# A mixture-of-experts block on one core: the light part of each unit first, halves in another order, and the last norm by token tile

## The chip, the cores and the metric

The kernel runs on one core of a Trainium2 chip. The metric is the device time of one execution in microseconds (us); the figure given for a kernel is the median of its runs.

## What is computed

One decoder block on 512 tokens of width 1024, in float32. A mixer (state-space branch and short convolution) comes first and is not touched here. Then each token goes to 8 of 64 experts and to one shared expert, and the sum is normalised:

```python
def moe_ffn(h, ...):
    scores = jax.nn.sigmoid((hf @ router_w).astype(jnp.float32))
    ...
    _, e_idx = lax.top_k(jnp.where(expert_mask, biased, -jnp.inf), TOP_K)
    ...
    def expert_block(args):
        xb, e = args
        return (jax.nn.silu(xb @ w_gate[e]) * (xb @ w_up[e])) @ w_down[e]
    ...
    return (routed + shared).reshape(b, s, d)

x = (layer_norm(ALPHA * x + g2 * ffn) * ln2_g[l] + ln2_b[l]).astype(dtype)
```

An expert has gate and up weights of 1024 x 256 each and down weights of 256 x 1024: 3 MB in all, and every expert is read once.

## The kernel before

**Blocks.** Experts are ranked by how many tokens they got, and each rank has a fixed capacity (CAPS). A block is 128 token slots. A *full* block belongs to one expert. Its products are made in three passes of a fast format (matmul3, lines 153 to 155): the weights are split into a high part, which ACT copies (L158), and a low part, which DVE subtracts (L160); the parts go into a ring of three sets (wset, wring). A *tile* block is shared by two or four experts, 64 or 32 slots each, and multiplies the unsplit weights in float32, one column tile of TensorE per expert (tiled, L950).

**Units.** A unit is a group of blocks handled together. Its kind is written as letters: y is an expert of 192 slots (a full block, and a tile block it shares with an expert of 64), z the same with 160 slots and one of 32, x one of 320 slots (two full blocks and a tile block), f a full block, a a tile block for one expert of 96 slots and one of 32, p a tile block for two of 64, q a tile block for four of 32. ORDER lists the units; each letter is a *part* of its unit (a list in subs).

**Inside a unit** (ffn). The gate and up product of a block is cut into two halves along the width of the model, because weights arrive in pieces of 1 MB: a piece is half of an expert's gate and up weights, or all of its down weights. halves_of gives the order of parts, blocks and halves:

```python
return [(s_, 0) for s_ in subs] + [(s_[::-1], 1) for s_ in subs[::-1]]
```

So unit ya does: first half of y's full block, of y's tile block, of a; then second half of a, of y's tile block, of y's full block. Four tile halves in a row stand between two full halves. After a block's second half, act_in (L927, L928) applies the SiLU on ACT and the product on DVE. Then come the transposes of the result, the combination matmuls of the unit before (csteps, L1188 and L1189, added to the residual by DVE at L1194), the transposes of the next unit's tokens, and the down products in the order of the blocks, each followed by done (L1161, L1165, and a split).

**Order of loads.** The loop over units plans the pieces in the order of the halves, with the down pieces of a unit last; SyncE's queue issues them in that order (L869, L872). A piece goes into one of seven pair slots in turn, and every eighth into another pool (expert_piece), so a piece takes over the slot of the piece eight before it, and its load waits until that one was used for the last time. Tokens are gathered by POOL (L1132), three buffers ahead.

**Order on the engines.** From unit 1 on, TensorE follows the order of the program (manual_schedule); the other engines' orders are made by the framework's scheduler.

**The end.** After the last unit, combine(True) adds the last parts: per token tile and half, two matmuls (L1188, L1189) and one DVE addition from PSUM that also sums the row (L1191). Then finish runs the last norm by the list FORD: square (q: the mean at L1483 on DVE, the squared sum at L1484 on ACT), root (r: L1488 on ACT, L1489 on DVE; for token tile 0 also L1491 on DVE and L1492 on ACT), scale (s: L1497 and L1498 on DVE, for token tile 0 L1501 and L1502 on POOL) and the store (L1503). A loop for tokens beyond the capacities follows; it runs zero times on these inputs.

Of the kernel before, what the change touches and what calls it, by code (L numbers as in the profile page):

```python
# [8 lines left out]
F32 = mybir.dt.float32  # L9
# [3 lines left out]
AF = mybir.ActivationFunctionType  # L13
OP = mybir.AluOpType
# [4 lines left out]
T, D, P = 512, 1024, 128  # L19
# [18 lines left out]
NXG = 3  # L38


ORDER = "x ya qy za ap ya qff za ya ap faa za ap faa p"
AHEAD = 10
NDEF = 2
FORD = "q0 r0 s0 q1 r1 s1 q2 r2 s2 q3 r3 s3"
NADA = 3
ENG3 = ("PP", "VV", "VV", "VV")
NWK = 5
# [16 lines left out]
def block_kernel(ctx: ExitStack, tc: tile.TileContext, a, out, dbg=None):  # L64
# [43 lines left out]
    def page(shape, dt=F32, pool=None):  # L108
        n = 1
        for q in shape:  # L110
            n *= q
        assert n == 1024
        if pool or not pw:
            return (pool or pa).tile([P, *shape], dt, name="pg", tag="pg")
        if not halves:
            t = pair([2, 1024], dt)
            halves.extend((t[:, 1], t[:, 0]))
        return halves.pop()
# [13 lines left out]
    def bc_rows(ap, n, parts=P):  # L132
        return bass.AP(tensor=ap.tensor, offset=ap.offset, ap=[[0, parts], [1, n]])
# [818 lines left out]

    def halves_of(subs):

        return [(s_, 0) for s_ in subs] + [(s_[::-1], 1) for s_ in subs[::-1]]

    def ffn(blocks, subs, xs, w, done, gp=False):

# [48 lines left out]
    ra = []  # L1007
# [170 lines left out]
    def csteps(last=False):  # L1178

        ps_ = list(parts)  # L1180
        parts.clear()
        for t in range(NT):
            for n in range(2):
                ns_ = slice(n * 512, (n + 1) * 512)
                o = bank("y", 2)
                for i, (oht, yh, yl) in enumerate(ps_):
                    oh_ = oht[:, t * P:(t + 1) * P]
                    PE.matmul(o, oh_, yh[:, ns_], start=(i == 0), stop=False)  # L1188
                    PE.matmul(o, oh_, yl[:, ns_], start=False, stop=(i == len(ps_) - 1))  # L1189
                if last:  # L1190
                    V.scalar_tensor_tensor(ra[t][:, ns_], ra[t][:, ns_], 1.0, o, op0=OP.mult, op1=OP.add,  # L1191
                                           accum_out=rsum[:, t, n:n + 1])
                else:
                    V.tensor_tensor(ra[t][:, ns_], ra[t][:, ns_], o, op=OP.add)  # L1194
                yield

    def combine(last=False):
        for _ in csteps(last):
            pass

    out_proj(0)
# [206 lines left out]
    def unit(n):  # L1410
# [16 lines left out]
        tail[0] = n + 1 == len(units)  # L1427
        drain(run)

    over_ = iter(())  # L1430
    need_x(1)
    for n in range(MAN):
# [3 lines left out]
    with tc.manual_schedule(engines={mybir.EngineType.PE}):  # L1436
        for n in range(MAN, len(units)):
            unit(n)
        combine(True)
    ostart, oend, obase, nov = far  # L1440


# [26 lines left out]
        V.tensor_copy(po, pof)  # L1469
        return po, pv, ei  # L1470

    ln2g, ln2b = page([D]), page([D])
    SY.dma_start(ln2g, bc_rows(a["ln2_g"], D))
    SY.dma_start(ln2b, bc_rows(a["ln2_b"], D))

    def finish():

        os_, st = {}, {}

        def square(t):  # L1480
            os_[t] = page([D])
            st[t] = const.tile([P, 4], F32, name="fst", bufs=4)
            V.tensor_scalar(st[t][:, 0:1], rsum[:, t, 0:1], rsum[:, t, 1:2], -1.0 / D, op0=OP.add, op1=OP.mult)  # L1483
            S.activation(os_[t], ra[t], AF.Square, bias=st[t][:, 0:1], scale=1.0, accum_out=st[t][:, 1:2])  # L1484

        def root(t):
            nmu, ss, rs, nb = (st[t][:, i:i + 1] for i in range(4))
            S.activation(rs, ss, AF.Sqrt, bias=epsc, scale=1.0 / D)  # L1488
            V.reciprocal(rs, rs)  # L1489
            if ENG3[t] != "VV":  # L1490
                V.tensor_tensor(nb, nmu, rs, op=OP.mult)  # L1491
                S.activation(os_[t], ra[t], AF.Identity, bias=nb, scale=rs)  # L1492

        def scale(t):
            o, nmu, rs = os_[t], st[t][:, 0:1], st[t][:, 2:3]
            if ENG3[t] == "VV":
                V.scalar_tensor_tensor(o, ra[t], nmu, ln2g, op0=OP.add, op1=OP.mult)  # L1497
                V.scalar_tensor_tensor(o, o, rs, ln2b, op0=OP.mult, op1=OP.add)  # L1498
            else:
                e1, e2 = ({"V": V, "P": GP}[e] for e in ENG3[t])  # L1500
                e1.tensor_tensor(o, o, ln2g, op=OP.mult)  # L1501
                e2.tensor_tensor(o, o, ln2b, op=OP.add)  # L1502
            SY.dma_start(out[0, t * P:(t + 1) * P, :], o)  # L1503

        for c in FORD.split():
            {"q": square, "r": root, "s": scale}[c[0]](int(c[1]))

    finish()
    nv = nc.values_load(nov[0:1, 0:1], min_val=0, max_val=E + 32)
    with tc.For_i(0, nv, 1):  # L1510
        po, pv, ei = overflow(ocur)
        er = nc.values_load(ei[0:1, 0:1], engines=[mybir.EngineType.SP], min_val=0, max_val=E - 1)
        blk = slots((pv[:, :, None], P, [po]))
        drain(expert([[0]], [[0]], [blk], [xsplit(blk[0])], lambda e, q: expert_piece(bass.ds(er, 1), q)))
        combine(True)
        finish()
        V.tensor_scalar(ocur, ocur, 1.0, None, op0=OP.add)

# [23 lines left out]
```

## Time and profile before

| what | us |
|---|---|
| median of 3 runs | 1582.76 |
| lowest, highest | 1582.29, 1587.55 |
| the profiled execution's own time | 1580.36 |
| its span, first to last instruction | 1578.6 |
| TensorE busy in the span | 1486.1 (94%) |
| VectorE busy | 975.3 (62%) |
| ScalarE busy | 644.8 (41%) |
| GpSimd busy | 227.3 (14%) |

The engines are named PE (TensorE's matmuls), PEld (its weight loads), DVE (VectorE), ACT (ScalarE), POOL (GpSimd) and SP (SyncE); a q behind a name is the engine's sequencer. Times in the trace are us from the start of the span. Matmuls are pipelined, so PE can count as busy while it is partly waiting; the start of one group to the start of the next is the safer measure. PEclk is the granted clock of TensorE as a share of its full 2.4 GHz.

### The profile page before, as it was taken

Reading aid. Unit: us, or ns where it says so; the run is one execution under the profiler, and the core shown is the slowest. Engines: PE = TensorE matmul, PEld = TensorE weight load, DVE = VectorE, ACT = ScalarE, POOL = GpSimd, SP = SyncE. Lnnn points to the kernel's source line nnn. Section 1 sums busy time; section 2 is a strip of 40 time slices with the busy share of each in tenths; the row PEclk is TensorE's granted clock in tenths of the full one; section 3 lists DMA queues with packets and bytes.
Section 4 is the critical chain, followed back from the end, with each engine's and each line's share of the span. In section 5 each row is a group of like instructions: output and inputs, shape, how many; then the busy total and the mean of one; then the engine's idle time right before and its main releaser. Section 6 shows DMA issues by size and latency. Waiting matters only on the chain.

```text
span 1578.6 us, 22869 instructions
## 1 busy us (share of the span) xinstructions
PE 1486.1 (94%) x8253; PEld 1010.2 (64%) x8253; DVE 975.3 (62%) x1810; ACT 644.8 (41%) x925; POOL 227.3 (14%) x232
## 2 busy tenths in 40 slices
PE   6999989999999999999988999999988999999994
PEld 3688777787787886788766455555555554454552
DVE  4457786678767666635696666454566544563456
ACT  3456665575643445523353333232343322231222
POOL 0011110111010445700023300000000000000001
PEclk9999999999999999999999999999999999999997
DMA  9763423632531557634622967998989788997871
GB/s 278 183 158 91 104 67 84 151 77 80 151 88 37 170 178 231 202 101 148 228 84 92 370 224 260 375 383 296 345 299 349 293 332 336 353 365 282 319 286 55
DMA packets 194504, 335.67 MB, mean 213 GB/s; under 512 B 13428, under 2 KB 136660, under 8 KB 186196
## 3 DMA queue, kind: packets, MB, share of 16 engines
q1 hardware_dynamic: 183300, 303.73, 55.6%
q0 software_dynamic: 11088, 30.45, 7.4%
q8 instruction: 66, 1.08, 0.3%
q14 instruction: 50, 0.41, 0.1%
HBM read 334.58 MB, written 4.28 MB: 215 GB/s over the span
## 4 chain that ended last, share of the span: by engine, by line
PE 73%; DMA 11%; DVE 8%; ACT 3%; issue 2%; POOL 1%; SPq 1%; DVEq 0%; ACTq 0%; POOLq 0%
PE ps_pj L153 12%; PE ps_pj L154 12%; PE ps_pj L155 12%; PE ps_pj L950 8%; DMA pr<-in_w_up_dram 8%; PE ps_y L950 5%; PE ps_y L1188 5%; PE ps_y L1189 5%; PE ps_tr L150 4%; DMA pg<-in_w_ada_dram 2%; DVE wl L160 2%; PE ps_y L153 1%; PE ps_y L155 1%; PE ps_y L154 1%; PE ps_y L483 1%
## 5 line engine op out<-in xcount | busy, mean ns | idle before, releaser
L153 PE MATMUL ps_pj<-hm,wh 128*128 128x512 f32 x680 | 276.5, 408 | 1.0 <-ACT wh L158 0.9
L155 PE MATMUL ps_pj<-hm,wl 128*128 128x512 f32 x680 | 267.7, 394 | 6.3 <-DVE wl L160 6.3
L154 PE MATMUL ps_pj<-hm,wh 128*128 128x512 f32 x680 | 267.7, 394 | 0.0
L160 DVE TENSOR_TENSOR wl<-pg,wh 128x1024 fp32r<-128x1024 f32 (+1 forms) x129 | 159.6, 1244 | 114.0 <-ACT wh L158 113.9
L950 PE MATMUL ps_pj<-pr,xt 128*32 128x512 f32 (+1 forms) x1472 | 214.2, 604 | 11.9 <-DMA pr<-in_w_up_dram 11.7
L158 ACT ACTIVATE wh<-pg 128x1024 fp32r<-128x1024 f32 (+1 forms) x135 | 127.5, 953 | 137.3 <-PE ps_pj L154 101.6
L950 PEld LDWEIGHTS ps_pj<-pr,xt 128*32 128x32 f32 (+1 forms) x1472 | 62.0, 117 | 153.2 <-issue 149.6
L153 PEld LDWEIGHTS ps_pj<-hm,wh 128*128 128x128 f32 x680 | 129.1, 190 | 36.3 <-issue 6.9
L155 PEld LDWEIGHTS ps_pj<-hm,wl 128*128 128x128 f32 x680 | 128.6, 189 | 35.9 <-DVE wl L160 8.1
L154 PEld LDWEIGHTS ps_pj<-hm,wh 128*128 128x128 f32 x680 | 128.8, 189 | 29.1 <-issue 3.4
L160 DVE TENSOR_TENSOR wl<-pr,wh 128x1024 fp32r<-128x1024 f32 x72 | 86.8, 1222 | 85.9 <-ACT wh L158 85.4
L1194 DVE TENSOR_TENSOR res<-res,ps_y 128x512 f32<-128x512 f32 x120 | 82.4, 687 | 76.0 <-PE ps_y L1189 74.4
L1132 POOL DMA_INDIRECT pg<-h_d,idx x41 | 45.4, 1107 | 559.6 <-DVE oht L1161 174.3
L158 ACT ACTIVATE wh<-pr 128x1024 fp32r<-128x1024 f32 x72 | 74.3, 1054 | 91.2 <-DMA pr<-in_w_up_dram 54.5
L950 PE MATMUL ps_y<-pr,wkr 128*32 128x512 f32 (+1 forms) x736 | 102.7, 596 | 1.3 <-DVE wk L1165 1.3
L927 ACT ACTIVATE sg<-ps_pj 128x256 f32<-128x256 f32 x44 | 16.8, 383 | 173.7 <-PE ps_pj L950 116.4
L928 DVE TENSOR_TENSOR sg<-sg,ps_pj 128x256 f32<-128x256 f32 x44 | 18.3, 420 | 111.8 <-ACT sg L927 111.8
L366 POOL TENSOR_TENSOR pg<-pg 128x1024 f32<-128x1024 f32 x28 | 73.8, 2650 | 56.9 <-ACT pg L364 56.8
L153 PE MATMUL ps_pj<-pg,wh 128*128 128x512 f32 x192 | 75.9, 395 | 1.1 <-ACT zs L431 1.1
L155 PE MATMUL ps_pj<-pg,wl 128*128 128x512 f32 x192 | 76.2, 397 | 0.0
L154 PE MATMUL ps_pj<-pg,wh 128*128 128x512 f32 x192 | 75.8, 395 | 0.0
L416 DVE SCALAR_TENSOR_TENSOR wk<-ps_pj,cw,wk 128x511 f32<-128x511 f32 (+2 forms) x93 | 68.3, 742 | 7.4 <-ACT wk L414 7.0
(394 smaller groups left out, 2658.5 us busy)
## 6 DMA issues: line engine op xcount, KB each, us to landing
pr<-in_w_gate_dram SPq DMA_DIRECT2D x128, 512.0 KB, 10.1
pr<-in_w_up_dram SPq DMA_DIRECT2D x128, 512.0 KB, 10.6
pr<-in_w_down_dram SPq DMA_DIRECT2D x64, 1024.0 KB, 9.6
pg<-in_w_in_dram SPq DMA_DIRECT2D x88, 512.0 KB, 6.4
pg<-in_w_ada_dram SPq DMA_DIRECT2D x48, 512.0 KB, 3.5
bc<-acs_d POOLq DMA_DIRECT2D x32, 256.0 KB, 4.1
pg<-in_w_ssd_out_dram SPq DMA_DIRECT2D x16, 512.0 KB, 4.4
pg<-in_w_sc_out_dram SPq DMA_DIRECT2D x8, 512.0 KB, 4.0
```

Source lines behind the costliest of these rows:

```text
L150: return PE.transpose(o, i, ident[:n, :n])
L153: PE.matmul(o, lh, rh, start=start, stop=False)
L154: PE.matmul(o, lh, rl, start=False, stop=False)
L155: PE.matmul(o, ll, rh, start=False, stop=stop)
L158: S.activation(hi, src, AF.Copy)
L160: V.tensor_tensor(lo, src, rw(hi), op=OP.subtract)
L366: GP.tensor_tensor(part[i], part[i], w, op=OP.add)
L416: V.scalar_tensor_tensor(acc[:, s:], o[:, :T - s], cw[:, 3 - s, tl:tl + 1], acc[:, s:], op0=OP.mult, op1=OP.add)
L950: PE.matmul(o[w * i:w * i + w, :], x[:, w * i:w * i + w], m, start=start, stop=stop, tile_position=(0, w * i))
L1188: PE.matmul(o, oh_, yh[:, ns_], start=(i == 0), stop=False)
L1189: PE.matmul(o, oh_, yl[:, ns_], start=False, stop=(i == len(ps_) - 1))
L1194: V.tensor_tensor(ra[t][:, ns_], ra[t][:, ns_], o, op=OP.add)
```

## The change

The letters of each unit are turned round, so that the tile-only part (a) comes first: ya, za and faa become ay, az and aaf; x, qy, ap, qff and p stay. halves_of turns the blocks of a part round in the first half instead of the second: unit ay now does a, y's tile block, y's full block; then y's full block, y's tile block, a. The plan of loads, the transposes of tokens and the down products follow the new order of blocks: in ay, a's down product comes first.

The last addition is no longer made whole before the norm: finish runs csteps itself, two steps (one token tile) per letter c of FORD. The loads of the norm's two vectors are issued on the first call of finish, ahead of the additions.

```diff
-ORDER = "x ya qy za ap ya qff za ya ap faa za ap faa p"
+ORDER = "x ay qy az ap ay qff az ay ap aaf az ap aaf p"
...
-FORD = "q0 r0 s0 q1 r1 s1 q2 r2 s2 q3 r3 s3"
+FORD = "c0 q0 r0 s0 c1 q1 r1 c2 q2 r2 s1 c3 q3 r3 s2 s3"
...
     def halves_of(subs):
 
-        return [(s_, 0) for s_ in subs] + [(s_[::-1], 1) for s_ in subs[::-1]]
+        return [(s_[::-1], 0) for s_ in subs] + [(s_, 1) for s_ in subs[::-1]]
...
-    def combine(last=False):
-        for _ in csteps(last):
-            pass
...
+    ln2 = []
+
+    def finish():
+
+        if not ln2:
+            for nm in ("ln2_g", "ln2_b"):
+                ln2.append(page([D]))
+                SY.dma_start(ln2[-1], bc_rows(a[nm], D))
+        ln2g, ln2b = ln2
+        com = csteps(True)
+        os_, st = {}, {}
+
+        def add(t):
+            next(com)
+            next(com)
...
+        for c in FORD.split():
+            {"c": add, "q": square, "r": root, "s": scale}[c[0]](int(c[1]))
...
         for n in range(MAN, len(units)):
             unit(n)
-        combine(True)
+        finish()
...
-        for c in FORD.split():
-            {"q": square, "r": root, "s": scale}[c[0]](int(c[1]))
-
-    finish()
     nv = nc.values_load(nov[0:1, 0:1], min_val=0, max_val=E + 32)
...
-        combine(True)
         finish()
```

square, root and scale are moved unchanged from behind the units to the new finish.

## Rows read from the trace of the kernel before

**Rows 1.** Busy time by stage: the routed experts, and the tail (windows view).

```profile
core 0: us, PE busy (x) PEld busy (x) DVE busy (x) ACT busy (x) POOL busy (x), PEclk, DMA share, GB/s
894.05:1532.82 638.77, 609.76 (x3952) 333.42 (x3951) 343.62 (x617) 190.08 (x300) 37.77 (x35) 0.99 0.85 323
1546.38:1571.58 25.20, 8.82 (x24) 3.54 (x20) 20.50 (x35) 9.24 (x17) 5.55 (x2) 0.72 0.11 45
```

**Rows 2.** What TensorE waited for in the expert stage: us, times, longest (waits view).

```profile
PE ps_pj L950 <- DMA pr<-in_w_up_dram: 11.7, 10, 2.3
PE ps_pj L154 <- DVE wl L160: 6.0, 7, 1.7
PE ps_pj L153 <- ACT wh L158: 3.2, 3, 1.4
```

**Rows 3.** Gate and up stretches of ten units, columns as in rows 1 (windows view).

```profile
980.54:1006.47 25.93, 23.34 (x124) 9.09 (x116) 7.59 (x9) 5.41 (x7) 0.00 (x0) 1.00 1.03 392
1033.61:1055.37 21.76, 20.72 (x154) 8.92 (x153) 6.71 (x13) 5.94 (x8) 0.00 (x0) 1.00 1.02 410
1079.59:1094.88 15.29, 15.15 (x101) 4.30 (x93) 2.59 (x5) 1.65 (x3) 0.00 (x0) 1.00 1.01 368
1163.16:1190.94 27.78, 22.95 (x117) 11.25 (x109) 12.34 (x13) 9.73 (x12) 0.00 (x0) 0.94 1.01 383
1217.66:1240.24 22.58, 20.15 (x154) 8.32 (x152) 9.86 (x16) 6.46 (x9) 0.00 (x0) 1.00 1.02 412
...
1310.46:1327.44 16.98, 15.15 (x100) 4.31 (x92) 2.46 (x4) 1.01 (x2) 0.00 (x0) 1.00 0.99 373
1349.80:1374.31 24.51, 21.03 (x154) 9.46 (x153) 6.30 (x9) 5.30 (x7) 0.00 (x0) 1.00 1.01 393
1396.56:1416.25 19.69, 19.69 (x157) 8.60 (x154) 6.58 (x10) 6.17 (x8) 0.00 (x0) 1.00 1.01 384
1440.43:1459.58 19.15, 16.85 (x101) 4.72 (x93) 2.59 (x5) 1.65 (x3) 0.00 (x0) 0.91 0.99 372
1481.65:1506.72 25.07, 22.62 (x155) 9.96 (x153) 7.35 (x9) 5.68 (x8) 0.00 (x0) 0.93 1.01 396
```

**Rows 4.** Four tile halves in a row in the za unit (timeline of TensorE).

```profile
1399.52 13.94 PE L950 MATMUL ps_pj<-pr,xt 128*32 128x512 f32 x128
```

**Rows 5.** What the queue of loads waited for longest in the expert stage (waits view, SP).

```profile
SPq L869 <- PE ps_y L950: 213.2, 25, 21.9
```

**Rows 6.** Down stage of the ya unit: start of the full block, tile blocks (timeline, TensorE).

```profile
1300.48 0.50 PE L153 MATMUL ps_y<-wh,wkr 128*128 128x512 f32 x1
...
1303.42 7.22 PE L950 MATMUL ps_y<-pr,wkr 128*64 128x512 f32 x48
```

**Rows 7.** The first load that this down stage lets go (timeline, SP).

```profile
1307.10 0.34 SPq L869 DMA_DIRECT2D pr<-in_w_gate_dram  x1
```

**Rows 8.** The opening full half of the za unit at 1217 (timeline, TensorE).

```profile
1219.80 0.50 PE L154 MATMUL ps_pj<-wl,xt 128*128 128x512 f32 x1 [1.75 <-DVE wl L160]
```

**Rows 9.** ACT and TensorE before the closing full half of the second faa (timelines).

```profile
1499.87 0.38 ACT L927 ACTIVATE sg<-ps_pj 128x256 f32<-128x256 f32 x1 [4.28 <-PE ps_pj L950]
1500.15 2.94 ACT L158 ACTIVATE wh<-pr 128x1024 fp32r<-128x1024 f32 x3
...
1501.25 0.50 PE L153 MATMUL ps_pj<-wh,xt 128*128 128x512 f32 x1 [1.42 <-ACT wh L158]
```

**Rows 10.** DVE's half of a weight split, with its mean of 1222 ns (page, part 5).

```profile
L160 DVE TENSOR_TENSOR wl<-pr,wh 128x1024 fp32r<-128x1024 f32 x72 | 86.8, 1222 | 85.9 <-ACT wh L158 85.4
```

**Rows 11.** Loads of up weights, median us from issue to landing (page, part 6).

```profile
pr<-in_w_up_dram SPq DMA_DIRECT2D x128, 512.0 KB, 10.6
```

**Rows 12.** DVE in the last norm: the last addition, the means, three passes (timeline).

```profile
1556.57 0.69 DVE L1191 SCALAR_TENSOR_TENSOR res<-res,ps_y 128x512 f32<-128x512 f32 x1
...
1557.18 0.57 DVE L1483 TENSOR_SCALAR fst<-rsum 128x1 f32<-128x1 f32 x4
1559.83 1.28 DVE L1497 SCALAR_TENSOR_TENSOR pr<-res,fst,pr 128x1024 f32<-128x1024 f32 x1 [2.08 <-ACT pr L1484]
...
1562.52 4.56 DVE L1497 SCALAR_TENSOR_TENSOR pr<-res,fst,pr 128x1024 f32<-128x1024 f32 x2
```

More of the change, by code (lines that the diff above doesn't have):

```diff
@@ L1428, in unit, with square, root, scale @@
         drain(run)
+    ln2 = []
[10 more added lines that the diff above has]
+            next(com)
+        def square(t):
+            os_[t] = page([D])
+            st[t] = const.tile([P, 4], F32, name="fst", bufs=4)
+            V.tensor_scalar(st[t][:, 0:1], rsum[:, t, 0:1], rsum[:, t, 1:2], -1.0 / D, op0=OP.add, op1=OP.mult)
+            S.activation(os_[t], ra[t], AF.Square, bias=st[t][:, 0:1], scale=1.0, accum_out=st[t][:, 1:2])
+        def root(t):
+            nmu, ss, rs, nb = (st[t][:, i:i + 1] for i in range(4))
+            S.activation(rs, ss, AF.Sqrt, bias=epsc, scale=1.0 / D)
+            V.reciprocal(rs, rs)
+            if ENG3[t] != "VV":
+                V.tensor_tensor(nb, nmu, rs, op=OP.mult)
+                S.activation(os_[t], ra[t], AF.Identity, bias=nb, scale=rs)
+        def scale(t):
+            o, nmu, rs = os_[t], st[t][:, 0:1], st[t][:, 2:3]
+            if ENG3[t] == "VV":
+                V.scalar_tensor_tensor(o, ra[t], nmu, ln2g, op0=OP.add, op1=OP.mult)
+                V.scalar_tensor_tensor(o, o, rs, ln2b, op0=OP.mult, op1=OP.add)
+            else:
+                e1, e2 = ({"V": V, "P": GP}[e] for e in ENG3[t])
+                e1.tensor_tensor(o, o, ln2g, op=OP.mult)
+                e2.tensor_tensor(o, o, ln2b, op=OP.add)
+            SY.dma_start(out[0, t * P:(t + 1) * P, :], o)
+        for c in FORD.split():
+            {"c": add, "q": square, "r": root, "s": scale}[c[0]](int(c[1]))
     over_ = iter(())
@@ L1470, in overflow @@
         return po, pv, ei
[L1472 to L1503, printed above, removed]
-        for c in FORD.split():
-            {"q": square, "r": root, "s": scale}[c[0]](int(c[1]))
-    finish()
     nv = nc.values_load(nov[0:1, 0:1], min_val=0, max_val=E + 32)
```

## The prediction

> **What bounds the kernel now.** I read the windows by stage first [rows 1]. From 894 us on, the routed experts take 638.8 us, with TensorE busy for 609.8 and the DMA engines for 85% of it; then comes a tail of 25.2 us in which TensorE does 8.8. An edit of order inside a unit can only win where TensorE waits, so the second view is the list of waits of TensorE over that stage [rows 2]: first for weights in transit (11.7 us, 10 times), then for the low part (6.0, 7 times) and the high part (3.2, 3 times) of a split full weight. These are gaps alone; pipelined matmuls hide part of what is lost, so the third view measures each unit's gate and up stretch [rows 3] against a clean one.
>
> A clean stretch is that of the za unit at 1396.56: two full and four tile halves in 19.69 us, all of it busy. Its four tile halves are one row of 13.94 us [rows 4], 3.49 each; a full half is (19.69 - 13.94) / 2 = 2.88. So the other stretches of [rows 3] should take 19.69 (qy at 980, za at 1033 and 1217, faa at 1349 and 1481), 13.94 (four tile halves: ap at 1079, 1310, 1440) and 4 x 2.88 + 6.97 = 18.49 (qff at 1163). They take 6.2, 2.1, 2.9, 4.8, 5.4, 1.4, 3.0, 5.2 and 9.3 us more: 40.3 in all. **That is all there is to win in these stretches.** In all of them the DMA share is about 1.0: the engines run flat out there, so what counts is when they were allowed to start.
>
> That is the fourth view, what the queue of loads waits for [rows 5]: 213.2 us for the down matmuls of tile blocks, 25 times. A weight piece lies in one of eight slots used in turn; the next unit's second halves go where this unit's down weights lie. In the ya unit at 1266 the down stage begins with the full block at 1300.48; its tile matmuls begin at 1303.42 and the y block is the first 16 of the 48 [rows 6]. The queue's next load leaves at 1307.10 [rows 7], when that block is done: two blocks into the stage.
>
> **The change, part by part.**
>
> 1. Light part first, so the light tile block is also the first of the down stage. The first two down slots come free after one tile block instead of a full and a tile block: earlier by the full block, 1303.42 - 1300.48 = 2.9 us [rows 6]. Six units are re-ordered like this (three ya, three za); behind them stand qy, ap, qff, ya, ap, ap, and of these the five that lost time in [rows 3] gain up to 2.9 each: qy 2.9, qff 2.9, ap 1.4, 2.9 and 2.9. The ap at 1440 also ran at a granted clock of 0.91 over 19.15 us, which is 1.7 us of half clock right behind its wait; with the wait I take that out too. Together 14.7. Bounds: 0 (the engines are busy anyway) and 25.1, the whole extra of the five.
>
> 2. Halves in the order tile, full, full, tile. The last tile half of a za unit asks for its weights a full half (2.9 us) later, which covers the 2.1 of the one at 1033. The one at 1217 opened with its full half and waited 1.75 us for its split [rows 8]; behind two tile halves (7 us) the split is long done: 2.9. Together 5.0; bounds 2 and 5.
>
> 3. The two faa units. The closing full half stands behind a SiLU that ACT can only run when the last tile half is done: SiLU at 1499.87, split from 1500.15, full matmul at 1501.25 after 1.42 us idle [rows 9]. In the new order the split follows the other full half, with no SiLU ahead of it. But the last piece of the unit is then asked for by a tile half that ends the stretch, and the wait for weights that stood in the fourth tile half is late next. Of 4.8 + 5.4 = 10.2 I take 6.2 as gone; bounds 3 and 10.2.
>
> 4. New: two full halves back to back need four split sets, and the ring has three. Each set feeds six matmuls, 1.44 us. The fourth split can start when the first set is used, takes 0.98 on ACT (2.94 for three [rows 9]) and 1.22 on DVE [rows 10], 2.2 in all, and two sets (2.88) are still ahead of TensorE: hidden. Bounds: 0, and 1.1 a pair, the mean wait for a high part in [rows 2], with ACT or DVE late. Nine pairs are new (six ay and az, two aaf, one in qy): 0 to 9.6; I take 3, nearer the hidden case, because no SiLU now stands between the two splits.
>
> 5. New: the unit opens with two tile halves that want four experts within 3.5 us, where a full half used to come between. In az behind qy, qff or aaf, two of these pieces get their slot only after the first down block, some 10 us before their use, and a load takes 10.6 from issue to landing [rows 11]. Bounds: 0, and three times the longest wait of 2.3 in [rows 2], 7; I take 2.
>
> 6. The end. Additions, norm and output go token tile by token tile instead of stage by stage. No instruction is added or removed. TensorE's order stays; DVE, ACT, POOL and the queue of SyncE get the same instructions in another order. The two loads of the norm's vectors are emitted ahead of the additions but stand behind the same weight loads on their queue; the whole last unit hides them, and without that cover they would cost their landing, 10.6. Before, the last addition starts at 1556.57, DVE then waits 2.08 us for ACT's first square, and of the six 1.28 us passes the two beside POOL's work took 4.56 [rows 12]. That idle time can be filled; some 1.3 us of small instructions move in between the additions. If POOL's 5.55 us [rows 1] slow DVE as before, the gain is 2.08 - 1.3 = 0.8; if they fall beside additions and slow nothing, the 2.0 us that the pair lost and as much for the second pair come on top: 4.8. I take 2.5. SyncE's stores keep their number, and the last one still ends the run.
>
> By the Trainium skill (SBUF — State Buffer, section "Who interferes with whom") a DVE instruction with two SBUF inputs is held up by a GpSimd one that reads SBUF, and one with a single SBUF input is not. The 4.56 us row agrees with the first half; no row here shows the second. By that rule the additions, which read PSUM, would be free beside POOL, and part 6 would be worth up to 4.8 instead of 2.5.
>
> Everything else (combination matmuls, gathers, transposes) keeps its count; only its blocks trade places.
>
> **Sum:** 14.7 + 5.0 + 6.2 - 3 - 2 + 2.5 = 23.4 us. The profiled execution took 1580.4, 2.4 below the median of the runs shown, so it would take 1557; the median, 1582.8 - 23 = **1560**.
>
> **The rivals.**
> - *The DMA engines are the bound in any order.* Their share is 1.0 in the slow stretches [rows 3], and an earlier start may only bring an earlier idle time. Then part 1 gives nothing: 23.4 - 14.7 = 8.7, 1574. Against it: 85% over the stage [rows 1], and a queue that waits 213 us for slots [rows 5].
> - *New waits eat the gain.* Parts 4 and 5 at their upper ends, 16.6 instead of 5, and part 1 halved: 23.4 - 11.6 - 7.4 = 4, about 1578. Here also belongs that DVE and ACT don't follow the written order: the manual order is TensorE's alone, and in [rows 12] the small instructions of four token tiles stand together although the list had them apart. Then part 6 is worth 0.
> - *Slower: the split becomes the pace of the full pair.* If each set waits for its own split, as at 1217, a full half costs 2.9 more [rows 3, 8], a pair 5.8, nine pairs 52: 1582.8 - 23.4 + 52 = 1611. It decides from (23.4 + 8) / 9 = 3.5 us a pair on. For it: a ring of three for four sets. Against it: the 2.2 us beside 2.88 of part 4.
>
> **Chances.** Forecast 0.58 (1549 to 1568), DMA bound 0.20 (1568 to 1578), eaten 0.14 (1575 to 1588), slower 0.08. What a measurement can tell from no change is about 0.5%, 8 us. Faster by more: 0.58 and most of the second, 0.15, so 0.73; same 0.19; slower 0.08. The range goes from 1549 (parts 3 to 6 at their good ends: 23.4 + 4 + 5 + 2.3 = 34.7, which is 1548, taken as 1549) to 1579, which leaves out the slower case, the end of the third and a little below.
>
> **What would show it.** Right: no wait for a high part ahead of the closing halves of aaf; the ap, qy and qff stretches shorter by some 3 us with the queue's loads leaving one block into the down stage; POOL's two passes beside the additions. Wrong: new gaps in front of the second full half (part 4), or of the second tile half of az (part 5), or loads that leave earlier and land no earlier (first rival).

## The result and the profile after

The changed kernel takes 1567.63 us (median of six runs, 1564.35 to 1569.95) against 1582.98 for the kernel before (six runs, 1582.29 to 1587.55): 15.4 us less, where 23 were forecast. The quotient of these medians is 0.9903; the ratio on record is 0.9886, with an interval of [0.9861, 0.9912] that holds both. One run of e2 below, 1684.91 us at a mean granted clock of 0.842, was in the chip's slow state and is left out. The profiled execution took 1568.29, with a span of 1566.5 against 1578.6: 12.1 less in the two executions that are compared line by line here.

The windows view comes first: nine of the ten stretches of [rows 3], columns as in [rows 1].

```profile
985.63:1014.18 28.55, 25.01 (x122) 9.30 (x121) 7.51 (x9) 6.04 (x8) 0.00 (x0) 0.88 0.99 379
1042.19:1063.28 21.09, 20.70 (x154) 8.67 (x152) 7.51 (x9) 6.04 (x8) 0.00 (x0) 1.00 1.01 403
1087.53:1101.67 14.14, 14.14 (x101) 4.06 (x93) 2.47 (x4) 1.13 (x3) 0.00 (x0) 1.00 0.95 350
1168.11:1193.31 25.20, 21.44 (x115) 11.24 (x113) 12.14 (x13) 9.75 (x12) 0.00 (x0) 1.00 1.00 370
1220.51:1241.72 21.21, 20.73 (x154) 8.68 (x153) 9.34 (x15) 5.93 (x8) 0.00 (x0) 1.00 1.01 394
1312.93:1327.09 14.16, 14.16 (x99) 4.08 (x97) 2.47 (x4) 1.06 (x3) 0.00 (x0) 1.00 0.97 374
1349.43:1371.22 21.79, 21.09 (x154) 8.54 (x152) 7.43 (x9) 5.47 (x8) 0.00 (x0) 1.00 1.02 379
...
1439.50:1453.63 14.13, 14.13 (x100) 4.06 (x92) 2.47 (x4) 1.13 (x3) 0.00 (x0) 1.00 1.00 363
1475.72:1496.82 21.10, 20.71 (x154) 8.62 (x153) 7.70 (x9) 5.88 (x8) 0.00 (x0) 1.00 1.01 387
```

Put each line beside its line in [rows 3]. The three ap stretches went from 15.29, 16.98 and 19.15 to 14.14, 14.16 and 14.13, all of it busy: they are clean now. The two faa stretches, now aaf, went from 24.51 and 25.07 to 21.79 and 21.10, the two az from 21.76 and 22.58 to 21.09 and 21.21. qff went from 27.78 to 25.20, and qy from 25.93 to 28.55. The ten together lost 17.7 us.

The waits view of TensorE over the expert stage shows what is new. It answers to [rows 2].

```profile
PE ps_pj L950 <- DMA pr<-in_w_up_dram: 9.0, 8, 2.1
PE ps_tr L150 <- ACT xt L911: 4.7, 6, 1.3
PE ps_y L153 <- DVE wk L1165: 2.7, 2, 1.4
PE ps_y L950 <- DVE wk L1165: 1.2, 1, 1.2
...
PE ps_pj L154 <- DVE wl L160: 0.2, 1, 0.2
```

Two lines of the same view of the kernel before:

```profile
PE ps_y L950 <- DVE wk L1165: 1.3, 3, 0.7
...
PE ps_tr L150 <- ACT xt L911: 0.8, 1, 0.8
```

The waits for a split weight in the gate and up stretches, 6.0 and 3.2 us in [rows 2], are down to 0.2. In their place stand waits that the prediction had no term for. They lie in the stretches between: TensorE waits for ACT's copy of transposed tokens (ps_tr, 4.7 us, 0.8 before) and for DVE's weighting of the down products (ps_y, L1165, 2.7 + 1.2 = 3.9 us, 1.3 before).

To follow the time in every run I divide the expert stage in the same way each time. A gate and up stretch runs from its first ps_pj matmul to the next product that is not one (15 of them); what lies between two of them (combination, transposes, down products) is the second sum (14); the end runs from the last stretch to the last instruction. Sums in us:

| kernel | gate and up | between | end |
|---|---|---|---|
| before | 304.4 | 334.3 | 45.8 |
| changed | 286.3 | 340.6 | 42.1 |
| e1 end alone | 304.0 | 334.5 | 42.1 |
| e2 down stage alone | 290.3 | 339.6 | 45.3 |
| e4 without turned halves | 282.1 | 339.9 | 42.3 |
| e5 without the new order of parts | 300.0 | 337.2 | 41.4 |
| e6 old order in the down stage | 291.1 | 336.5 | 42.6 |
| e8 q part last | 295.1 | 334.4 | 42.3 |
| e9 fewer bytes in qy and qff | 275.1 | 338.6 | 42.3 |
| e10 changed, again | 284.5 | 339.5 | 42.2 |
| e11 one step fewer ahead | 282.5 | 334.4 | 42.5 |

So of the two profiled executions: 18.1 gained in the gate and up stretches, 6.3 lost between them, 3.7 gained at the end, and 3.5 lost ahead of the expert stage, which begins at 897.52 instead of 894.05. Whether the change has a part in these 3.5 us stays open. The turned halves do alter the order in which the framework places the work just ahead of the stage (TensorE's instructions come in another order from 816 us on). But the start moves as much between executions with one and the same order there: from 894.1 to 902.0 us in the three with that of the kernel before (before, e1, e2), and from 894.1 to 901.8 in the eight with that of the changed kernel. I therefore leave the 3.5 us out of the change's price; without them 18.1 - 6.3 + 3.7 = 15.5, close to the 15.4 between the medians.

### The profile page after: what moved, and what is told of

It reads as the page before. It is cut to its first block, busy times and chain, and to the rows that moved or that the text cites. A ratio compares the mean times of both kernels' runs of the same rounds, so it can differ in the third digit from the quotient of the medians.

```text
span 1566.5 us, 22861 instructions
## 1 busy us (share of the span) xinstructions
PE 1484.3 (95%) x8253; PEld 1008.4 (64%) x8253; DVE 971.2 (62%) x1810; ACT 644.9 (41%) x925; POOL 228.1 (15%) x232
## 3 DMA queue, kind: packets, MB, share of 16 engines
q8 instruction: 66, 1.08, 0.3%
## 4 chain that ended last, share of the span: by engine, by line
PE 75%; DMA 10%; DVE 8%; ACT 3%; issue 2%; POOL 1%; SPq 1%; ACTq 0%; DVEq 0%; POOLq 0%
PE ps_pj L153 12%; PE ps_pj L155 12%; PE ps_pj L154 12%; PE ps_pj L950 10%; DMA pr<-in_w_up_dram 6%; PE ps_y L950 5%; PE ps_y L1188 5%; PE ps_y L1189 5%; PE ps_tr L150 4%; DMA pg<-in_w_ada_dram 2%; PE ps_y L153 1%; DVE wl L160 1%; PE ps_y L155 1%; PE ps_y L154 1%; POOL pg L366 1%
## 5 line engine op out<-in xcount | busy, mean ns | idle before, releaser
L150 PE MATMUL ps_tr<-ident,pg 128*128 128x128 f32 x392 | 64.3, 288 | 9.9 <-ACT xt L911 5.4
```

Source lines behind the costliest of these rows:

```text
L150: return PE.transpose(o, i, ident[:n, :n])
```

## The experiments

**e1, the end alone** (the changed kernel with the old order and the old halves):

```diff
-ORDER = "x ay qy az ap ay qff az ay ap aaf az ap aaf p"
+ORDER = "x ya qy za ap ya qff za ya ap faa za ap faa p"
...
-        return [(s_[::-1], 0) for s_ in subs] + [(s_, 1) for s_ in subs[::-1]]
+        return [(s_, 0) for s_ in subs] + [(s_[::-1], 1) for s_ in subs[::-1]]
```

> Only the end is changed (additions, norm and store by token tile); order of units and halves as before. Theory: the end is worth what the two traces differ by from the end of the last unit's second tile half to the last instruction, 45.8 before and 42.0 after, so 42 here, and about 1579 in all. Rival: part of that difference came from what lies before the end, and the end is worth the 2.5 that the prediction took: 43.3. The ten stretches of rows 3 should keep their lengths within 2 us each under both.

Measured: one time, 1584.3, beside 17 runs of the kernel before on that chip (median 1585.4, 1575.8 to 1591.6). The end is 42.1 against 45.8: 3.6 us shorter, and the other two sums are those of before. Single stretches repeat less well: the ap at 1310 in [rows 3], 16.98, is 15.22 here with nothing changed in it. One time can't show 3.6 us; the trace can. Three lines of DVE at the end of the changed kernel (timeline) say how it came:

```profile
1549.38 0.67 DVE L1191 SCALAR_TENSOR_TENSOR res<-res,ps_y 128x512 f32<-128x512 f32 x1
...
1549.97 2.88 DVE L1460 SCALAR_TENSOR_TENSOR pr<-pr,fst 128x1024 f32<-128x1024 f32 x1
...
1552.97 3.17 DVE L1459 SCALAR_TENSOR_TENSOR pr<-res,fst,pr 128x1024 f32<-128x1024 f32 x1
```

And POOL's two passes in the same kernel (timeline):

```profile
1549.43 2.35 POOL L1463 TENSOR_TENSOR pr<-pr 128x1024 f32<-128x1024 f32 x1 [83.08 <-ACT pr L1454]
1551.86 3.20 POOL L1464 TENSOR_TENSOR pr<-pr 128x1024 f32<-128x1024 f32 x1
```

The last addition (L1191, one input in PSUM) ran beside POOL in 0.67, as fast as without it [rows 12]. The two passes beside POOL took 2.88 and 3.17 instead of 1.28. Only one of the eight additions ended up beside POOL, where the good end of part 6 had counted on them; what is gone is DVE's wait of 2.08 us for ACT's first square [rows 12], since additions now stand where DVE was idle. By the Trainium skill (SBUF — State Buffer, "Who interferes with whom") a DVE instruction with two SBUF inputs is held up by a GpSimd one that reads SBUF, and one with at most one SBUF input is not, outside DVE's 2-port modes; these lines agree with both halves, the 0.67 with the one that no row of before showed.

The ends of the passes speak for a standstill of DVE rather than a slower pass: POOL's two passes end at 1551.78 and 1555.06, and DVE's two end 1.07 and 1.08 us after them, a little less than the 1.28 of a whole pass. The kernel before has the same pattern, 1.08 both times.

**e5, the halves alone** (the changed kernel with the old order of parts; the new end stays):

```diff
-ORDER = "x ay qy az ap ay qff az ay ap aaf az ap aaf p"
+ORDER = "x ya qy za ap ya qff za ya ap faa za ap faa p"
```

> The changed kernel with the old order of units (ya, za, faa), so only the halves inside a part are turned, and the end. Theory: early slots come from the order of units, so the waits for weights are as before: ap stretches 15 to 19, faa 24 to 25 (its parts have one block each, so nothing in it is turned), qy and qff as before; the za at 1217 loses its wait for a split, 22.6 to 20 or 21. Sum over the ten stretches 36 to 40 above clean, about 1577 to 1580 in all. Rival: turning the halves is worth half of the change; then the ap and za stretches are near 14.1 and 20 here.

Measured: one time, 1583.3 (before on that chip: median 1585.0). Windows of the second za, a faa and an ap:

```profile
1229.09:1249.12 20.03, 20.03 (x153) 8.20 (x152) 10.53 (x16) 6.25 (x9) 0.00 (x0) 1.00 1.02 415
...
1357.35:1383.40 26.05, 22.61 (x154) 10.61 (x153) 7.36 (x9) 5.29 (x7) 0.00 (x0) 0.93 1.01 400
1449.85:1467.13 17.28, 15.14 (x100) 4.30 (x92) 2.57 (x5) 1.65 (x3) 0.00 (x0) 1.00 1.02 369
```

The za stretch that opened with a wait for its split is clean (20.03 against 22.58 in [rows 3]). The first za went from 21.76 to 21.06. The faa stretches stay as long as before (26.05 and 24.71). The ap stretches stay above the 14.14 of the changed kernel, at 15.09, 15.38 and 17.28; the last is shorter than its 19.15 in [rows 3], but that one had a granted clock of 0.91 and this one 1.00. Turning the halves brings 3.2 of the 5.0 us of part 2, and nothing for the ap and faa stretches.

**e4, the new order of parts without turned halves:**

```diff
-        return [(s_[::-1], 0) for s_ in subs] + [(s_, 1) for s_ in subs[::-1]]
+        return [(s_, 0) for s_ in subs] + [(s_[::-1], 1) for s_ in subs[::-1]]
```

> The changed kernel with the old order of halves: the light part first, but the full half ahead of the tile half in the first half, and behind it in the second (in ay: tile, full, tile, tile, full, tile). Theory: the early slots come with the order of units, so the ap stretches are 14.1 as in the changed kernel; the waits for a split ahead of aaf's closing full half go too, since a tile half of a now closes the unit; 1567 to 1571. Rival: the pair of full halves side by side is what matters; then the waits for weights and splits come back by half or more, 1573 to 1578.

Measured: 1568.61, ratio 0.9896 [0.9871, 0.9920]: the time of the changed kernel. Windows of qy and the two aaf:

```profile
989.52:1014.62 25.10, 22.30 (x123) 9.78 (x121) 7.42 (x9) 5.66 (x8) 0.00 (x0) 1.00 0.97 374
...
1350.41:1371.95 21.54, 20.88 (x154) 8.54 (x152) 7.48 (x9) 5.47 (x8) 0.00 (x0) 1.00 1.02 387
1476.73:1497.10 20.37, 20.37 (x154) 9.01 (x153) 7.69 (x9) 5.87 (x8) 0.00 (x0) 1.00 1.02 390
```

The whole gain in the stretches is in the order of the parts. With the light part first, old halves do as well: the pattern "tile, full, full, tile" is not worth anything that can be measured beside it, and qy is shorter without it (25.10 against 28.55). The aaf gain needs no turned halves either: each part of aaf has a single block, so both patterns give tile, tile, full, full, tile, tile, the last half is a tile half, and no split stands behind the SiLU.

**e2, light part first in the down stage alone** (the kernel before, with the down products and the down loads of ya, za and faa in the turned order, which a new function down_of gives; all else as before):

```diff
-        for i, b in enumerate(blocks):
-            ah, al = acts[i]
+        for i in down_of(blocks, subs):
+            b, (ah, al) = blocks[i], acts[i]
...
```

> The kernel before, with one thing moved: in the ya, za and faa units the down products, and the loads of the down weights, begin with the light part a; gate and up halves stay as before. Theory (slots): two slots come free one full block earlier, so the three ap stretches fall from 15.3, 17.0 and 19.2 to about 14.1, while qy (25.9), qff (27.8), za (22.6) and faa (24.5, 25.1) stay within 1.5; new waits in the down stages give 2 to 5 back: 1575 to 1579. Rival (order of demand): the ap waits went because the halves ask for their weights in another order; then the ap stretches stay at 15 to 19 here and the time at 1582.

Measured: 1579.63 (median of nine runs), ratio 0.9958 [0.9933, 0.9982], 5.8 us less than before on that chip. Windows of qy, ap, qff, the other two ap and the second faa, in order of time:

```profile
988.53:1013.75 25.22, 22.55 (x122) 9.11 (x121) 7.42 (x9) 5.94 (x8) 0.00 (x0) 1.00 0.99 375
1086.85:1100.99 14.14, 14.14 (x101) 4.06 (x93) 2.47 (x4) 1.13 (x3) 0.00 (x0) 1.00 0.98 356
1169.84:1195.19 25.35, 21.40 (x115) 11.21 (x113) 11.97 (x13) 10.19 (x12) 0.00 (x0) 1.00 1.00 373
1317.61:1331.77 14.16, 14.16 (x99) 4.08 (x97) 2.47 (x4) 1.01 (x2) 0.00 (x0) 1.00 1.00 362
...
1445.47:1460.44 14.97, 14.97 (x100) 4.31 (x92) 2.47 (x4) 1.14 (x3) 0.00 (x0) 1.00 0.97 366
1482.51:1504.39 21.88, 21.12 (x155) 8.75 (x154) 5.16 (x7) 3.76 (x6) 0.00 (x0) 1.00 1.00 395
```

This is part 1 by itself, and it shows both its sides. The ap waits are gone without any other edit (14.97 in the third, without idle time): slots that come free one full block earlier are the cause, as far as the down products and the order of the down loads, which move together here, can be taken as one. qy and qff do not become clean. The second faa was expected to stay within 1.5 of its 25.07 and fell to 21.88, so the early slots shorten it too. And the sum between the stretches has already risen, from 334.3 to 339.6: a loss belongs to this edit as well, though not the waits for ACT's copy (ps_tr), which stand at 0.8 here as before.

**e6, the counter-test** (the changed kernel; ay, az and aaf do their down products and down loads with the full block first):

```diff
-        for i, b in enumerate(blocks):
-            ah, al = acts[i]
+        for i in down_of(blocks, subs):
+            b, (ah, al) = blocks[i], acts[i]
...
```

> The changed kernel with one thing undone: the down products and down loads of ay, az and aaf begin with the full block again, and a comes last. Theory: the late slots are back, so the ap stretches go from 14.1 back to 15 to 19 and the time rises by 6 to 10, while the stretches between gate and up stages fall from 340.6 to about 335; net 1569 to 1573. The gains that come from demand (aaf 21 to 22, az 20 to 21.5) stay. Rival: demand inside the unit is all; then the ap stretches stay at 14.1 and the kernel is 5 us faster than the changed one.

Measured: 1569.99, ratio 0.9914 [0.9881, 0.9948]. Windows of an ap, an aaf and another ap:

```profile
1310.38:1326.96 16.58, 15.14 (x100) 4.30 (x93) 2.45 (x4) 1.01 (x2) 0.00 (x0) 1.00 1.00 376
1349.33:1371.25 21.92, 20.73 (x154) 8.58 (x152) 7.61 (x9) 6.65 (x10) 0.00 (x0) 1.00 1.01 383
1438.73:1455.96 17.23, 15.14 (x100) 4.30 (x92) 2.58 (x5) 1.65 (x3) 0.00 (x0) 1.00 1.01 370
```

The ap waits are back (16.58 and 17.23), the aaf gain stays, and the sum between the stretches falls to 336.5, by 4.1 against the first profile of the changed kernel and by 3.0 against the second (e10). The wait for ACT's copy stays at 4.7. The two sides of part 1 nearly cancel: the time can't be told from that of the changed kernel.

**e8, the q part last in its units**, so that the weights of the six-expert units' light part are asked for later:

```diff
-ORDER = "x ay qy az ap ay qff az ay ap aaf az ap aaf p"
+ORDER = "x ay yq az ap ay ffq az ay ap aaf az ap aaf p"
```

> The changed kernel with q behind its partners: units yq and ffq in place of qy and qff. Theory (slots): in qy and qff the second halves of q's four experts take the slots of q's own first halves, so their loads can't leave before the unit's first 3.5 us are over; with q in the middle, two of the four leave before that, and the two stretches, 28.6 and 25.2 with 8.9 and 6.7 above clean, fall to 4 to 6 above clean each: 1561 to 1566. Rival: the rate of the loads is the bound there, six experts' weights in one unit; then the waits only change place and both stay 6 to 9 above clean, 1567.

Measured: 1569.21, ratio 0.9895 [0.9849, 0.9942]. Windows of yq, the az behind it, and ffq:

```profile
979.37:1009.33 29.96, 24.12 (x123) 8.99 (x119) 7.71 (x10) 5.81 (x8) 0.00 (x0) 0.94 1.01 380
1036.30:1063.30 27.00, 23.63 (x156) 9.09 (x148) 7.70 (x9) 5.51 (x7) 0.00 (x0) 0.87 1.01 383
1167.76:1196.33 28.57, 23.15 (x114) 11.89 (x113) 12.29 (x18) 8.90 (x11) 0.00 (x0) 0.94 1.01 386
```

Neither six-expert stretch became shorter, and the az behind yq became longer (27.00 against 21.09). All gate and up stretches together are 8.8 us longer, those between them 6.2 shorter, and the time is that of the changed kernel. The granted clock, 0.94, 0.87 and 0.94, has a part in the three lengths. The DMA share stays at 1.0 in all three.

**e9, fewer bytes in the six-expert units.** The second gate and up pieces of part q in qy and qff load two of their four rows, and the matmuls of that half use these two rows twice: 4 MB less to load, the same matmuls.

```diff
-                SY.dma_start(r[:, i], w.rearrange("(p k) n -> p k n", k=KD)[:, 4 * q:4 * q + 4, :])
+                SY.dma_start(r[:, i, :nk], w.rearrange("(p k) n -> p k n", k=KD)[:, 4 * q:4 * q + nk, :])
...
+            if lite and e < 4 and q in (2, 3):
+                return held[e][:, :, 0:2, :]
...
```

> The changed kernel, but in qy and qff the second gate and up pieces of q's four experts are loaded by half (the first two rows of each four; the matmuls of the second half use these rows twice, so the outputs are not the block's). Eight pieces lose 0.5 MB each; slots, waits and matmuls stay. Theory (rate): the tail of qy and qff waits for bytes, not for slots: with 2 MB less between the first half of q and the second, 5 us at some 400 GB/s, qy's and qff's 8.9 and 6.7 above clean fall to 0 to 3; 1559 to 1562. Rival (slots): the loads leave too late, when the slots come free, and a load's way is what is waited for; then both stay within 2 us of what they were.

Measured: one time, 1552.16. Windows of qy and qff:

```profile
980.92:1002.15 21.23, 21.00 (x122) 8.66 (x121) 7.51 (x9) 6.01 (x8) 0.00 (x0) 1.00 0.96 354
1156.77:1177.41 20.64, 20.32 (x114) 11.10 (x112) 12.24 (x13) 9.80 (x12) 0.00 (x0) 1.00 0.98 351
```

28.55 and 25.20 became 21.23 and 20.64, against 19.69 and 18.49 for clean ones. In these two units the rate of the loads is the bound: six experts' weights in a stretch whose matmuls take no longer than those of a four-expert unit. Of the 4 MB half belongs to each unit, and 2.1 MB at the 370 GB/s of qff are 5.7 us; 4.6 came. Part of qy's gain is the granted clock, 1.00 here and 0.88 in the changed kernel. Fewer bytes help in these units, an earlier start does little.

**e3 and e7, the split of the down weights earlier and later.** In the down stage of aaf, DVE does the split ahead of the weighting that TensorE waits for, as three lines of the changed kernel show (timelines of DVE, then of TensorE):

```profile
1385.86 2.35 DVE L160 TENSOR_TENSOR wl<-pr,wh 128x1024 fp32r<-128x1024 f32 x2
1388.13 1.40 DVE L1165 SCALAR_TENSOR_TENSOR wk<-ps_y,red,pg 128x512 f32<-128x512 f32 x2
```

```profile
1388.92 3.64 PE L950 MATMUL ps_y<-pr,wkr 128*32 128x512 f32 x32 [1.15 <-DVE wk L1165]
```

e3 writes the split ahead of the token transposes:

```diff
-        yield
         us = [{e: w(e, 4 + j) for e in es} for j in range(2)]
         wdn = {e: [split(us[j][e], GP if gp else None) for j in range(2)] for e in split_e}
+        yield
...
-        zipper(xs_steps(i2), com, islice(over_, 1))
         next(run)
+        zipper(xs_steps(i2), com, islice(over_, 1))
```

> The changed kernel, with the split of the full block's down weights written ahead of the next unit's token transposes instead of behind them. Theory: the low part of that split (two of 1.2 us on DVE) stands ahead of the scaling of the down products, which holds TensorE 1.15, 1.39 and 1.30 us in two aaf units and qff; written earlier, these gaps go, and the stretches between gate and up stages shrink by 3 to 6 us in all: 1562 to 1565. Rival: DVE is full in the down stage whatever the order; the gaps stay and the time too, 1567.6.

Measured: 1569.17, ratio 0.9905 [0.9876, 0.9934]; between the stretches 340.2. But the edit didn't reach DVE: in aaf its split still stands right ahead of the weighting (timeline of e3):

```profile
1386.97 2.35 DVE L160 TENSOR_TENSOR wl<-pr,wh 128x1024 fp32r<-128x1024 f32 x2
1389.24 1.40 DVE L1165 SCALAR_TENSOR_TENSOR wk<-ps_y,red,pg 128x512 f32<-128x512 f32 x2
```

The order written out by hand is TensorE's alone, so this run tells nothing of the cause. e7 goes the other way, with aaf's split behind the first down block:

```diff
...
+        late = len(blocks) == 3 and len(blocks[0]) == 4 and len(blocks[1]) == 4
+        if not late:
+            split_down()
         for i, b in enumerate(blocks):
+            if late and i == 1:
+                split_down()
```

> The changed kernel with the split of the down weights of aaf's full block written behind the first block's scaling instead of ahead of it; nothing else moves. Theory: the two low parts on DVE, 2.35 us, hold the scaling that frees TensorE's banks; with the split behind it the gaps of 1.15 and 1.39 us in the two aaf down stages go, and the stretches from aaf to the next unit fall from 24.3 and 20.6 to about 23 and 19.3. Rival: the gaps come from DVE being full; they only move to the full block, and the two stretches stay within 0.4.

Measured: one time, 1569.84; between the stretches 339.8; the two stretches behind aaf took 23.74 and 20.62 (24.25 and 20.62 in the changed kernel). Again the edit reached DVE only in part. In the first aaf one of the two low parts now stands behind the first weighting (low parts at 1389.54 and 1391.34, the weighting at 1390.68), and the gap went from 1.15 to 0.47. In the second aaf both low parts still stand ahead of the weighting that TensorE waits for (1512.96 and 1514.70, ahead of 1515.84), and the gap stayed at 1.4. So the gap shrank where a low part moved out of the way and not where none did. That fits the theory, but two gaps do not show it, and how much the rest of DVE's work costs there stays open.

**e10, the changed kernel again,** on the same chip as e9 and e11, to see how far the sums repeat.

> The changed kernel itself, on this chip beside the others. Theory: ap stretches 14.1, aaf 21 to 22, qy 25 to 29 and qff 25, the stretches between about 340, the end 42; 1566 to 1570, with the start of the expert stage anywhere from 894 to 903, which no edit here touches. Rival: the stretches that the theory calls settled move by more than 1 us from one execution to the next, and the account by stretches means little.

Measured: 1566.51, ratio 0.9886 [0.9839, 0.9932]. The three sums lie within 1.8 us of the first profile's, and no single gate and up stretch differs by more than 0.9 us. Between them one does by 1.6: the one behind x, 22.87 in the first profile at a granted clock of 0.93, 21.26 here at 1.00.

**e11, one combination step fewer ahead of the activation transposes.** The list of TensorE's work in a unit gives two combination steps first and the others between transposes. In the changed kernel the last token transposes of a unit stand with no product between them, and the last four wait for a copy. With one step fewer at the head, one more is left for the end:

```diff
-        for _ in range(2):
-            next(com, None)
+        next(com, None)
```

> The changed kernel with one combination step instead of two ahead of the transposes of the unit's results, so that one more step is left to stand between the transposes of the next unit's tokens. Theory: TensorE's wait of about 0.7 us for ACT's copy of the last token transposes (4.7 us in all) comes from the steps having run out; with one more left it goes, and the stretches between sum to 336 or less: 1563 to 1566. Rival: the first of the two steps hides the SiLU and the product of the last block; without it TensorE waits there instead, 1567 to 1572.

Measured: **1561.13** (six runs, 1558.0 to 1562.5), ratio 0.9858 [0.9812, 0.9903]; e10 on the same chip took 1566.51. The sum between the stretches is 334.4 against 339.5 in e10. It equals that of before only by balance: behind the two aaf it is still 0.9 and 1.7 us longer and behind the az at 1233 1.0, in others shorter. Token transposes of one unit in the timeline of the changed kernel:

```profile
1256.17 0.71 PE L150 MATMUL ps_tr<-ident,pg 128*128 128x128 f32 x4
1257.57 0.71 PE L150 MATMUL ps_tr<-ident,pg 128*128 128x128 f32 x4 [0.69 <-ACT xt L911]
```

in that of e11, and then in that of the kernel before:

```profile
1247.84 1.16 PE L150 MATMUL ps_tr<-ident,pg 128*128 128x128 f32 x8
```

```profile
1254.59 1.25 PE L150 MATMUL ps_tr<-ident,pg 128*128 128x128 f32 x8
```

and the waits view of e11:

```profile
PE ps_y L153 <- DVE wk L1165: 4.3, 5, 1.5
...
PE ps_tr L150 <- ACT xt L911: 0.7, 1, 0.7
```

Eight transposes run through where four waited for a copy; this wait fell from 4.7 to 0.7 us. In the kernel before, the last eight stood without a product between them too and did not wait, so the missing product is not the whole cause: the order of tile and full blocks has a part in it that no run here takes apart. The one for L1165 stays (4.3 us in the row above, 2.7 in that of the changed kernel), the next thing to look at. This version beats both kernels.

## Why the prediction was right, and where not

The direction was right and 1567.6 lies in the range; 15.4 us came of the 23.4 summed. The mechanism was right for the ap and faa stretches; the terms for qy, for qff and for the full pair were mis-sized, and one term was missing. Step by step:

**Part 1, earlier slots (14.7 forecast).** The mechanism is shown, by e2 (alone, the ap waits go) and e6 (taken back, they return). In the unit of [rows 6] and [rows 7] the first load now leaves 3.7 us into the down stage instead of 6.6; from the timeline of TensorE, then that of SP:

```profile
1302.80 3.64 PE L950 MATMUL ps_y<-pr,wkr 128*32 128x512 f32 x32
```

```profile
1306.49 0.34 SPq L869 DMA_DIRECT2D pr<-in_w_gate_dram  x1
```

The three ap stretches gave 1.2, 2.8 and 5.0, 9.0 in all, where 1.4 + 2.9 + 4.6 = 8.9 was forecast. (Against e1, whose three ap have the code of before and took 15.28, 15.22 and 19.24, it is 7.3.) The step that failed is "qy 2.9, qff 2.9". Compared at the same granted clock of 1.00, qy took 25.93 before and 25.10 to 25.40 in e2, e3 and e4: 0.5 to 0.8, and at most 1.5 against e1's 26.58, the same code as before. For qff, 27.78 in [rows 3] has a clock of 0.94, and so has e4's qff with 26.42; that makes 1.4, and the rest of its 2.6 comes with the clock. The first rival, the rate of the loads in any order, was true of these two units (e9; e8 agrees), while the ap stretches followed the slots. It could have been read from [rows 3]: their DMA share was 1.0 over the longest stretches, and they are the two with six experts.

**The clock in qy.** In the changed kernel's own profile qy was longer than before, 28.55. Windows of 3 us inside it:

```profile
1004.00:1007.00 3.00, 1.02 (x2) 0.14 (x2) 0.00 (x0) 0.00 (x0) 0.00 (x0) 0.97 1.02 423
1007.00:1010.00 3.00, 2.31 (x12) 0.69 (x16) 0.00 (x0) 0.00 (x0) 0.00 (x0) 0.50 1.03 431
```

and three lines of TensorE's timeline, two in qy and one in aaf:

```profile
1005.13 1.02 PE L950 MATMUL ps_pj<-pr,xt 128*32 128x512 f32 x2 [2.00 <-DMA pr<-in_w_up_dram]
1007.69 6.56 PE L950 MATMUL ps_pj<-pr,xt 128*32 128x512 f32 x26 [1.54 <-DMA pr<-in_w_up_dram]
...
1367.70 3.59 PE L950 MATMUL ps_pj<-pr,xt 128*32 128x512 f32 x26 [0.62 <-DMA pr<-in_w_up_dram]
```

Two waits for weights, 2.00 and 1.54, and TensorE busy for 1.02 of 3 us; then a granted clock of 0.50, the lower of its two levels (1.2 of 2.4 GHz). The last 26 tile matmuls took 6.56 us; the same number in aaf took 3.59. So 3.0 us of the stretch are the clock's. The turned halves go with it: of the seven profiles in which qy has them and all its loads (changed, e3, e5, e6, e7, e10, e11) its granted clock was 0.88 to 0.94 in six and 1.00 in e3 alone, and qy took 25.40 to 28.60; in the four with the old halves (before, e1, e2, e4) it was 1.00 each time, and qy took 25.10 to 26.58. The pair of full halves in qy, which part 4 priced as a wait for splits, took 5.68 there like the others, so the new order seems to cost qy by way of the clock. Why the clock falls in the turned order and not in the old one, no run shows.

**Part 2 and part 5, the az units (5.0 - 2 = 3 forecast).** 0.7 and 1.4 came, 2.0. The wait for the split went; waits for weights of 0.39 and 0.48 in the opening tile halves came, as part 5 said. The turned halves were not needed for it: in e4, with the old ones, the two az took 20.05 and 20.72.

**Part 3, the faa units (6.2 forecast).** 2.7 and 4.0 came, 6.7. Some of the 4.0 is the clock: the second faa had 0.93 in [rows 3], and the aaf has 1.00. No wait for the closing split is left, and the wait for weights in the last tile half is the one "late next": 0.62 in the line at 1367.70, 0.39 in the second aaf. e4 shows that the order of the parts, not of the halves, did it; e6, that the order of demand alone is enough (21.92 and 20.17), and e2, that early slots alone do most of it in the second (21.88).

**Part 4, the full pair (-3 forecast, and the slower rival).** Almost nothing: eight of the nine pairs took 5.66 to 5.69 us, against 2 x 2.88 = 5.76, and the first aaf's 6.16. The split is hidden, as its working said. The price that I put on it was caution. The count of nine left out x, whose four full halves now stand in a row; they took 11.11, against 4 x 2.88 = 11.52.

**The term that was missing: -6.3 between the stretches.** "Everything else (combination matmuls, gathers, transposes) keeps its count; only its blocks trade places" was the sentence that failed: the count held, the time did not. Of the 6.3 us, 1.5 is the granted clock of 0.93 behind x, which e10 does not repeat. For the rest two waits can be named.

First, the token transposes of a unit now come in another order of tile and full blocks, and the last of them wait for a copy: 4.7 us in the changed kernel and also in e6, whose down products have the old order, against 0.8 in before, e1, e2 and e5. So this wait comes with the order of the parts. With one product more between the transposes (e11) it is 0.7, and the sum between the stretches 5.1 us shorter than in e10.

Second, in the down stages of the two aaf DVE's weighting is late, and TensorE waits 1.15 and 1.39 us for it. e2 and e6 show that the order of the down blocks is a cause of a longer time between the stretches (5.3 up; 3.0 to 4.1 down). That the bank of a full block comes free late because ACT and then DVE read it is only argued. The second rival had the sign of such a loss, though it looked for it in parts 4 and 5.

**Part 6, the end (2.5 forecast).** 3.7, and 3.6 in e1. Filling DVE's idle time was the right mechanism: from its first L1191 to its last pass DVE took 22.4 us before and takes 19.3 now, with 4.0 and 1.5 of them idle. The 1.3 us charged for small instructions did not come due, since they stand where DVE had waited. That POOL's work would fall beside additions, the way to more than 0.8, was wrong. The prediction also misread the row of 4.56 in [rows 12]: it is one pass of 1.28 ahead of POOL's work and one of 3.36 beside it. POOL held up two passes before (3.36 and 3.17) and holds up two now (2.88 and 3.17), 0.5 us less. The last 0.5 us of the gain lies behind DVE's last pass.

Sum: 9.0 (ap) + 0 (qy and qff, -2.6 and +2.6 with the clock) + 2.0 + 6.7 + 0.4 in the other five stretches = 18.1; less 6.3, plus 3.7.

## What to carry to other kernels

When blocks trade places, walk the whole round of the pipeline once more, past the stage that the edit is for: who reads the buffer that the moved block fills, and how much other work stands between it and the next use. Before a wait for loads is put down to a late start, look at whether the stretch asks for more bytes than its matmuls' time can bring; an earlier start helps only where it doesn't. And compare stretches at the same granted clock, but then ask whether the change itself brings the clock down.

## What was not expected of the hardware

The expert stage began at 894.1, 901.7 and 902.0 us in three executions with the same instructions in the same order up to there (before, e2, e1): a single profile can't show a gain below some 8 us by its span, only by its stretches. In the tail DVE seems to have waited for POOL where their passes met: in the changed kernel DVE's two passes took 2.88 and 3.17 us instead of 1.28 and ended 1.07 and 1.08 us after POOL's, while the addition from PSUM took 0.67 in the same place. POOL's second pass took 3.20, its first 2.35; the second began 1.0 us before DVE's pass ended, which fits a wait on that side too, but no run has POOL's passes by themselves.
